# Softmax weights of a windowed attention: transposes on TensorE, or in blocks on VectorE with a way over DRAM

## The chip, the cores and the metric

The kernel runs on one core of a Trainium2 chip. The metric is the device time of one execution in microseconds (us). Lower is better.

## What is computed

One layer of a hybrid decoder block on 2048 tokens of width 1024, all in float32. A normalized input goes through one wide projection. One branch is a gated causal convolution of width 3. The other is attention over a sliding window of 128 tokens, with 16 query heads that share 4 key and value heads of 64 channels, and a learned sink for each head. Cut to the attention:

```
scores = einsum('bnqhgd,bnkhd->bnhgqk', qb, kb) * scale      # blocks of 128 queries, 256 keys
scores = where(valid, scores, NEG_INF)                       # 0 <= q_pos - k_pos < 128
m = maximum(max(scores, axis=-1), sink)
p = exp(scores - m)
p = p / (sum(p, axis=-1) + exp(sink - m))
out = einsum('bnhgqk,bnkhd->bnqhgd', p, vb)
```

Both branches are gated, projected and merged with sigmoid gates; an output projection and the residual follow.

## The kernel before

The tokens are worked in two tiles of 1024. In each tile the projections come one after the other: keys, values, queries, then the convolution's columns and its gate factor (the convolution stage), the merge gates (the gate stage), the two SiLU gates, and the projections of the two branches `ya` and `yb`. The output projection comes at the end. Each product is split into float32r high and low parts and summed on TensorE, with a scheme of sums that saves products, so a "unit" of 256 columns takes seven groups of 12 matmuls.

**Ticks.** Everything else hangs on these groups. The generators (`sunit`, `qunit`, `branch`) yield after each group, and `run` (L601) counts a tick for each yield. `put(n, f)` places a function at tick `n`. After each group `run` issues the next loads of weights, the high half of a piece of weights (ScalarE), the first two functions of the tick, the low half (VectorE), and then the rest of the tick's functions. Every engine works its own list strictly in the order in which this host program issues it. The order is fixed when the kernel is built; nothing is moved afterwards.

**An attention step** handles one of 4 key heads, one block of 128 queries, and the 4 query heads that belong to it. There are 32 steps in a token tile, 64 in all. Each has a place `n`, and `attention` (L1461) puts its parts at fixed distances from it:

- `att_load` (n - 4): SP loads queries `q`, keys `kq` and their low parts `lows`.
- `att_scores` (n): six matmuls into the one score buffer `s` (two PSUM banks), then masking and the row maximum on VectorE.
- `att_exp` and `att_load_v` (n + 1): exponentials on ScalarE, and the load of the values `v` by SP.
- `att_norm` (n + 2): VectorE divides by the sums. `p` now lies with the queries on the partitions.
- `att_turn` (n + 4): TensorE turns the four 128 by 128 blocks of `p` into the PSUM tile `pt` (L966). ScalarE copies `pt` twice (`xh` L969, `yp` L970), VectorE subtracts `xl = pt - xh`, and GpSimd cuts the window's triangles with four selections (`keep`, L979).
- `att_values` (n + 7): six matmuls with the values into `po` (L996).
- `att_out` (n + 8): ScalarE and VectorE add the halves in PSUM to `o` (L1007), and SP stores it.

The places of the first 16 steps are 5.25 ticks apart (rounded down) from the 48th tick of a token tile, and those of the other 16 are 3.25 ticks apart from the 129th. In the first token tile the convolution stage takes ticks 46 to 129 and the gate stage 130 to 185; the second token tile begins at tick 305.

**Buffers.** Most of these tiles come from one pool of 19 slots, `big`, each of 512 float32 for each partition (`slot`); a new tile takes a slot that became free, and its first writer waits for the last reader of the old one. `pt` and `po` come from three PSUM banks (`mbank`), which other transposes use too. GpSimd also issues DMAs (`nc.gpsimd.dma_start`); the other loads and stores are issued by SP in order.

VectorE's `transpose` is already in use in the query stage (`ptq<-q_t`), where it turns a 128 by 512 tile within blocks of 32 by 32.

Of the kernel before, what the change touches and what calls it, by code (L numbers as in the profile page):

```python
# [8 lines left out]
F32 = mybir.dt.float32  # L9
# [6 lines left out]
P = 128  # L16
# [8 lines left out]
G = NH // NKV  # L25
HD = 64
# [25 lines left out]
QUADS = [slice(32 * k, 32 * k + 32) for k in range(4)]  # L52

PE_TURNS = ((0, 0), (0, 1))
TURN_WAIT = 3
HALVES = (LH, UH)


@with_exitstack
def block_kernel(  # L60
# [12 lines left out]
    nc = tc.nc  # L73
# [16 lines left out]
    dram = ctx.enter_context(tc.tile_pool(name="dram", bufs=1, space=bass.MemoryType.DRAM))  # L90

    def slot(shape, dt, name):
        return big.tile(shape, dt, tag="big", name=name)
# [7 lines left out]
    def mbank(name):  # L101
        return ps_m.tile([P, HB, P], F32, tag="m", name=name)
# [31 lines left out]
    ident = consts.tile([P, P], F32, name="ident")  # L134
# [5 lines left out]
    for h in range(2):  # L140
        nc.gpsimd.affine_select(
            out=mask_f[:, h, :], in_=ones[:, 0:HD], pattern=[[1, HD]], compare_op=ALU.is_gt,
# [74 lines left out]
    vec = Woven()  # L217
# [23 lines left out]
    def add(o, a, b, eng=None):  # L241
        return (eng or vec).tensor_tensor(out=o, in0=a, in1=b, op=ALU.add)
# [355 lines left out]
    def put(n, f):  # L598
        at.setdefault(max(n, tick[0] + 1), []).append(f)

    def run(gen):  # L601
        while True:
            tick[0] += 1
            if next(gen, gen) is gen:
                tick[0] -= 1
                return
            ahead_loads()
            hi, lo = (piece() if tick[0] >= W_FROM else None) or (None, None)
            if hi:
                hi()  # L610

            fs = at.pop(tick[0], [])
            for f in fs[:2]:
                f()
            if lo:
                lo()
            for f in fs[2:]:
                f()
            vec.some(WOVEN)

# [338 lines left out]
        mul(p, p, st[:, 0].unsqueeze(2).to_broadcast([P, G, P]))  # L959
        return p  # L960

    def att_turn(t, j, b, p):
        nm = f"{t}_{j}_{b}"
        pt = mbank(f"pt{nm}")
        for i in range(G):
            nc.tensor.transpose(pt[:, i, :], p[:, i, :], ident)  # L966
        xh, xl = slot([P, G, P], F32R, f"xh{nm}"), slot([P, G, P], F32R, f"xl{nm}")
        y = slot([P, G, P], F32R, f"yp{nm}")
        nc.scalar.copy(xh, pt)  # L969
        nc.scalar.copy(y[LH], pt[UH])  # L970
        vec.tensor_tensor(out=xl, in0=pt, in1=xh.bitcast(F32), op=ALU.subtract)

        def keep(dst, src, prev):
            sg = 1 if prev else -1
            d4 = dst.rearrange("p g (e q) -> p (g e) q", q=HD)
            s4 = src.rearrange("p g (e q) -> p (g e) q", q=HD)
            nc.gpsimd.affine_select(  # L979
                out=d4, in_=s4, pattern=[[0, 2 * G], [-sg, HD]],  # L980
                compare_op=ALU.is_gt if prev else ALU.is_ge, fill=0.0, base=0,
                channel_multiplier=sg)

        keep(xh[UH], xh[UH], False)
        keep(y[LH], y[LH], True)
        keep(y[UH], xl[UH], True)
        keep(xl[UH], xl[UH], False)
        return xh, xl, y

    def att_values(t, j, b, pcv, v2):  # L990
        xh, xl, y = pcv
        po = mbank(f"po{t}_{j}_{b}").rearrange("p g q -> p (g q)")
        for h in range(2):
            cs = slice(h * 2 * P, (h + 1) * 2 * P)
            for n, (kind, xx) in enumerate(((2 + h, xh), (h, y), (2 + h, xl))):
                nc.tensor.matmul(  # L996
                    po[:, cs], lhsT=v2[:, kind, :], rhs=xx.rearrange("p g q -> p (g q)")[:, cs],
                    start=n == 0, stop=n == 2)
        return po

    def att_out(t, j, b, po):
        pov = po.rearrange("p (h c e q) -> p h c e q", h=2, c=2, e=2)
        o = slot([P, 2, P], F32, f"o{t}_{j}_{b}")
        for e in range(2):
            own, oth = HALVES[e], HALVES[1 - e]
            ov = o[own].rearrange("p c (h q) -> p h c q", h=2)
            nc.scalar.copy(ov, pov[oth, :, :, e, :])  # L1007
            add(ov, pov[own, :, :, e, :], ov)
        nc.sync.dma_start(
            od[t][2 * j : 2 * j + 2, :, b * P : (b + 1) * P].rearrange("c p q -> p c q"), o)  # L1010

# [449 lines left out]
    def attention(t, places):  # L1461
        for r, n in enumerate(places):
            j, b = divmod(r, NB)
            got = {}

            def step(k, f, got=got):
                def g():
                    got[k] = f(got)
                return g

            put(n - 4, step("l", lambda g, j=j, b=b: att_load(t, j, b)))
            put(n + 1, step("v", lambda g, j=j, b=b: att_load_v(t, j, b)))
            put(n, step("s", lambda g, j=j, b=b: att_scores(t, j, b, g["l"])))
            put(n + 1, step("e", lambda g, j=j, b=b: att_exp(t, j, b, g["s"])))
            put(n + 2, step("n", lambda g: att_norm(g["e"])))
            put(n + 4, step("x", lambda g, j=j, b=b: att_turn(t, j, b, g["n"])))
            put(n + 7, step("o", lambda g, j=j, b=b: att_values(t, j, b, g["x"], g["v"])))
            put(n + 8, step("z", lambda g, j=j, b=b: att_out(t, j, b, g["o"])))

    def next_tile(t, n0):  # L1480

# [53 lines left out]
    for t in range(NT):  # L1535
        ops = state[t]["ops"]
        ys, yc, opa, opb = {}, {}, {}, {}
        t0 = tick0
        if t == 0:
            t0 += 1  # L1540
        attention(t, [t0 + 48 + int(5.25 * r) for r in range(16)] + [
            t0 + 129 + int(3.25 * r) for r in range(16)])
        if t > 0:
            run(sunit(("k", t), ops, fin_k(t)))
            run(sunit(("v", t), ops, fin_v(t)))
        for j in range(NKV):
            if t == j == 0:
                run(qunit(("q", t, j), ops, fin_q(t, j)))
            else:
                run(sunit(("q", t, j), ops, fin_q(t, j), t == 0 and j < Q_TWO))  # L1550
        for k in range(KC):
            run(sunit(("cv", t, k), ops, fin_cv(t, k, ys)))
            if k % 2:
                run(sunit(("b", t, k // 2), ops, fin_b(t, k // 2, ys)))
        for w, key in enumerate(("ga", "gb")):
            for j in range(NJ):
                run(sunit((key, t, j), ops, fin_g(t, w, j)))

        def use_o(k, q, o):
            nc.sync.dma_start(ocd[t][k, :, hs(q)], o)  # L1560

        def oa_form(k, q):
            opa[k, q] = split_op(yc[k, q], f"opa{t}_{k}_{q}")

        def use_y(k, q, y):
            yc[k, q] = y
            if k >= KC - 2:
                oa_form(k, q)

        zs = [("za", j) + fin_z(t, j, od[t], "za", use_o) for j in range(NJ)]  # L1570
        zs += [("z", j) + fin_z(t, j, yd[t], "z", use_y) for j in range(NJ)]
        zs[0][3]()
        for n, (key, j, fin, _) in enumerate(zs):
            if n + 1 < len(zs):
                put(tick[0] + 4, zs[n + 1][3])
            else:

                for i, (k, q) in enumerate([(k, q) for q in (1, 0) for k in range(KC - 2)]):
                    put(tick[0] + 1 + i // 2, lambda k=k, q=q: oa_form(k, q))
            run(sunit((key, t, j), ops, fin))  # L1580
        n0 = tick[0]
        for n, (k, q) in enumerate((k, q) for q in range(2) for k in range(KC)):
# [74 lines left out]
```

## Time and profile before

| | us |
|---|---|
| median of 3 runs (lowest to highest) | 1988.09 (1986.5 to 1989.5) |
| the profiled execution | 1987.95 |
| its span, first to last instruction | 1986.2 |
| TensorE busy in it | 1964.9 (99%) |
| VectorE busy | 1407.5 (71%) |
| ScalarE busy | 927.4 (47%) |
| GpSimd busy | 379.4 (19%) |

The profile is of one execution. PE is TensorE's matmuls, PEld its weight loads, DVE is VectorE, ACT is ScalarE, POOL is GpSimd and SP the engine that issues most DMAs; SPq is its queue. A line such as `L966 PE MATMUL pt<-ident,p` names the source line, the engine, the operation, and what is written from what. Behind it stand the shapes, the count, the busy time, the mean duration in nanoseconds and the idle time ahead of it with what ended it. In a timeline the first two columns are the start and the duration, or for several merged instructions the stretch that they take. Matmuls are pipelined: the next one starts before the last one's recorded end, so the pitch from start to start is what TensorE spends on one. A window row gives the stretch, its length, each engine's busy time and count, TensorE's granted clock, the share of the DMA engines and their GB/s.

### The profile page before, as it was taken

To read this page: it belongs to the slowest core of one execution; us is meant where nothing else is said; L and a number is where in the kernel's file an instruction comes from. 1 tells how busy PE (TensorE), PEld (TensorE's weight loads), DVE (VectorE), ACT (ScalarE), POOL (GpSimd) and SP (SyncE) were. 2 spreads that over 40 slices of the span, in tenths; PEclk is the share of its full clock that TensorE was granted. 3 is DMA by queue.
4 is the path that set the end of the run, shared out by engine and by line. 5 is a ranking of instruction groups with operands and counts; after the bars stand their busy time and mean duration, and the time that the engine had idled before them with its cause. 6 is when DMAs were issued, how large, how long until landed. Compare 5 with 4: busy or idle time off the path is not lost.

```text
span 1986.2 us, 27039 instructions
## 1 busy us (share of the span) xinstructions
PE 1964.9 (99%) x9102; PEld 1631.9 (82%) x9102; DVE 1407.5 (71%) x2428; ACT 927.4 (47%) x1860; POOL 379.4 (19%) x530
## 2 busy tenths in 40 slices
PE   9999999999999999999999999999999999999999
PEld 7877888888888888888878888887888888888887
DVE  7988788787775554379689778876776565356654
ACT  7655545556664343324555544555664334222321
POOL 2372122223230000110463222222321000100000
PEclk9999999999999999999999999999999999999999
DMA  8484543465555435774584544364654524855553
GB/s 295 109 221 124 154 125 112 133 185 184 174 158 201 137 110 185 265 270 143 144 216 136 154 119 123 117 189 155 200 181 162 185 96 157 271 190 172 163 175 112
DMA packets 204059, 332.95 MB, mean 168 GB/s; under 512 B 24144, under 2 KB 98896, under 8 KB 203920
## 3 DMA queue, kind: packets, MB, share of 16 engines
q1 hardware_dynamic: 189696, 288.96, 45.7%
q0 software_dynamic: 14080, 42.22, 7.9%
q8 instruction: 73, 1.20, 0.3%
q14 instruction: 66, 0.54, 0.1%
q10 hardware_dynamic: 144, 0.03, 0.0%
HBM read 234.39 MB, written 96.73 MB: 167 GB/s over the span
## 4 chain that ended last, share of the span: by engine, by line
PE 82%; DVE 7%; ACT 4%; DMA 3%; issue 2%; POOL 1%; SPq 0%; DVEq 0%; ACTq 0%; POOLq 0%
PE Y L410 26%; PE yb L1126 9%; PE ya L1126 8%; PE Vcv L410 4%; PE Xcv L410 4%; PE Vb L410 2%; PE Xb L410 2%; PE Xz L410 2%; PE Xza L410 2%; PE Vo L410 2%; PE Xo L410 2%; PE Vza L410 2%; PE po L996 2%; PE Vz L410 2%; PE Xgb L410 2%
## 5 line engine op out<-in xcount | busy, mean ns | idle before, releaser
L979 POOL TENSOR_SCALAR_AFFINE_SELECT xh<-xh 64x512 fp32r<-64x512 f32 x64 | 70.6, 1103 | 652.3 <-DVE xl L211 499.6
L950 ACT ACTIVATE p<-s,st,rq 128x128 f32<-128x128 f32 x256 | 113.3, 453 | 0.5
L211 DVE TENSOR_TENSOR o<-po,o 64x256 f32<-64x256 f32 x128 | 53.7, 420 | 58.0 <-ACT o L1007 55.7
L211 DVE SCALAR_TENSOR_TENSOR tha<-tha,ya 128x512 f32<-128x512 f32 x32 | 22.0, 687 | 97.6 <-PE ya L1126 94.6
L1007 ACT COPY o<-po 64x256 f32<-64x256 f32 x128 | 46.9, 367 | 83.8 <-DVE o L211 82.3
L211 DVE TENSOR_TENSOR xl<-pt,xh 128x512 fp32r<-128x512 f32 x64 | 44.2, 691 | 53.9 <-ACT yp L970 48.4
L1126 PE MATMUL ya<-opa,wya_1h 128*128 128x512 f32 x256 | 79.6, 391 | 0.9 <-ACT opa L238 0.5
L410 PE MATMUL Xcv<-oph,wcv_ah 128*128 128x512 f32 x256 | 79.7, 392 | 0.0
L1126 PE MATMUL yb<-opb,wyb_1h 128*128 128x512 f32 x256 | 78.9, 389 | 0.0
L1126 PE MATMUL yb<-opb,wyb_0h 128*128 128x512 f32 x256 | 78.9, 389 | 0.0
L1126 PE MATMUL ya<-opa,wya_0h 128*128 128x512 f32 x256 | 78.8, 389 | 0.0
L238 ACT CAST opb<-ocr 128x512 fp32r<-128x512 f32 x32 | 19.9, 621 | 110.6 <-DMA ocr<-ocd 109.0
L1126 PEld LDWEIGHTS ya<-opa,wya_1h 128*128 128x128 f32 x256 | 48.0, 188 | 12.2 <-ACT opa L238 1.3
L1126 PEld LDWEIGHTS ya<-opa,wya_0h 128*128 128x128 f32 x256 | 48.0, 188 | 10.0
L1126 PEld LDWEIGHTS yb<-opb,wyb_1h 128*128 128x128 f32 x256 | 48.0, 188 | 9.9
L1126 PEld LDWEIGHTS yb<-opb,wyb_0h 128*128 128x128 f32 x256 | 48.0, 188 | 9.9
L410 PEld LDWEIGHTS Xcv<-oph,wcv_ah 128*128 128x128 f32 x256 | 47.2, 188 | 9.3
L979 POOL TENSOR_SCALAR_AFFINE_SELECT yp<-xl 64x512 fp32r<-64x512 f32 x64 | 54.0, 844 | 3.1
L211 DVE SCALAR_TENSOR_TENSOR thb<-thb,yb 128x512 f32<-128x512 f32 x32 | 21.9, 686 | 43.7 <-PE yb L1126 43.0
L211 DVE SCALAR_TENSOR_TENSOR y<-u,cols,y 128x512 f32<-128x512 f32 x64 | 49.1, 767 | 5.4 <-ACT y L1038 4.2
L969 ACT CAST xh<-pt 128x512 fp32r<-128x512 f32 x64 | 37.5, 586 | 32.5 <-PE pt L966 31.7
L1214 POOL DMA_DIRECT2D wo<-in_w_out x16 | 8.7, 541 | 225.0 <-DVE opb L211 205.6
(590 smaller groups left out, 6260.2 us busy)
## 6 DMA issues: line engine op xcount, KB each, us to landing
wcv_raw<-in_w_in SPq DMA_DIRECT2D x32, 512.0 KB, 4.4
q<-q2d SPq DMA_DIRECT2D x64, 256.0 KB, 3.9
v<-vd SPq DMA_DIRECT2D x128, 128.0 KB, 3.3
gd<-th SPq DMA_DIRECT2D x64, 256.0 KB, 2.3
wq_raw<-in_w_in SPq DMA_DIRECT2D x16, 512.0 KB, 5.2
q2d<-q_h POOLq DMA_DIRECT2D x64, 128.0 KB, 4.7
q2d<-q_l POOLq DMA_DIRECT2D x64, 128.0 KB, 4.6
kq<-q2d SPq DMA_DIRECT2D x128, 64.0 KB, 3.6
```

The source lines that it names most:

```text
L211: r = f(*args, **kw)
L238: nc.scalar.copy(hi, src)
L410: nc.tensor.matmul(ps, lhsT=w[:, j, :], rhs=b[:, m, :], start=start and j == 0 and i == 0, stop=j == KP - 1 and i == 2, skip_group_check=n ...
L950: nc.scalar.activation(out=p[:, i, :], in_=sg[:, i, HD : 3 * HD], func=AF.Exp, bias=st[:, 1, i : i + 1], scale=rv[:, i // 2, i % 2 : i % 2 ...
L969: nc.scalar.copy(xh, pt)
L979: nc.gpsimd.affine_select(out=d4, in_=s4, pattern=[[0, 2 * G], [-sg, HD]], compare_op=ALU.is_gt if prev else ALU.is_ge, fill=0.0, base=0, ...
L996: nc.tensor.matmul(po[:, cs], lhsT=v2[:, kind, :], rhs=xx.rearrange("p g q -> p (g q)")[:, cs], start=n == 0, stop=n == 2)
L1007: nc.scalar.copy(ov, pov[oth, :, :, e, :])
L1126: nc.tensor.matmul(ps, lhsT=w[:, j, cs], rhs=o[:, m, :], start=n == 0 and i == 0, stop=n == KC - 1 and i == 2)
L1214: nc.gpsimd.dma_start(h, w_o[c * P : (c + 1) * P, hs(q)])
```

## The change

The four TensorE transposes of `att_turn` go. In their place come two new steps. `att_flip` lets VectorE turn `p` into `f` within blocks of 32 by 32, with the four heads side by side in each block row, and GpSimd sends `f` to DRAM. `att_back` lets GpSimd read it back with four DMAs, one for each 32 partitions, in such an order that the blocks change places and `x` has the keys on the partitions. `att_turn` then works on `x` in SBUF instead of `pt` in PSUM. The columns of `x` are ordered by block of 32 queries, head and query, and the patterns in `keep`, `att_values` and `att_out` follow that order.

The steps get new distances: loads at n - 5, block transpose at n + 2, the way back at n + 5, the value loads at n + 6, `att_turn` at n + 9, the value matmuls at n + 13, the output at n + 14. The places change as well: in the convolution stage 0, 6, 10 and 15 ticks into every 21, in the gate stage 3.75 ticks apart. And `run` issues one function of a tick ahead of the low half of weights instead of two.

```diff
+V_, F_, B_, X_, O_ = 6, 2, 5, 9, 13
...
             fs = at.pop(tick[0], [])
-            for f in fs[:2]:
+            for f in fs[:1]:
                 f()
             if lo:
                 lo()
-            for f in fs[2:]:
+            for f in fs[1:]:
                 f()
...
+    def att_flip(t, j, b, p):
+        nm = f"{t}_{j}_{b}"
+        f = slot([P, G * P], F32, f"f{nm}")
+        vec.transpose(out=f, in_=p.rearrange("p g (b r) -> p b g r", r=32))
+        fd = dram.tile([P, G * P], F32, name=f"fd{nm}")
+        nc.gpsimd.dma_start(fd, f)
+        return fd
+
+    def att_back(t, j, b, fd):
+        x = slot([P, G, P], F32, f"x{t}_{j}_{b}")
+        src = fd.rearrange("(a r) (b x) -> b r a x", a=4, b=4)
+        for k in range(4):
+            nc.gpsimd.dma_start(x[QUADS[k]], src[k])
+        return x
+
+    def att_turn(t, j, b, pt):
+        nm = f"{t}_{j}_{b}"
-        pt = mbank(f"pt{nm}")
-        for i in range(G):
-            nc.tensor.transpose(pt[:, i, :], p[:, i, :], ident)
...
-                out=d4, in_=s4, pattern=[[0, 2 * G], [-sg, HD]],
+                out=d4, in_=s4, pattern=[[0, 2], [-32 * sg, 2], [0, G], [-sg, 32]],
...
-                    po[:, cs], lhsT=v2[:, kind, :], rhs=xx.rearrange("p g q -> p (g q)")[:, cs],
+                    po[:, cs], lhsT=v2[:, kind, :], rhs=xx[:, :, h * HD : (h + 1) * HD],
...
-            put(n - 4, step("l", lambda g, j=j, b=b: att_load(t, j, b)))
-            put(n + 1, step("v", lambda g, j=j, b=b: att_load_v(t, j, b)))
+            put(n - 5, step("l", lambda g, j=j, b=b: att_load(t, j, b)))
+            put(n + V_, step("v", lambda g, j=j, b=b: att_load_v(t, j, b)))
...
-            put(n + 4, step("x", lambda g, j=j, b=b: att_turn(t, j, b, g["n"])))
-            put(n + 7, step("o", lambda g, j=j, b=b: att_values(t, j, b, g["x"], g["v"])))
-            put(n + 8, step("z", lambda g, j=j, b=b: att_out(t, j, b, g["o"])))
+            put(n + F_, step("f", lambda g, j=j, b=b: att_flip(t, j, b, g["n"])))
+            put(n + B_, step("b", lambda g, j=j, b=b: att_back(t, j, b, g["f"])))
+            put(n + X_, step("x", lambda g, j=j, b=b: att_turn(t, j, b, g["b"])))
+            put(n + O_, step("o", lambda g, j=j, b=b: att_values(t, j, b, g["x"], g["v"])))
+            put(n + O_ + 1, step("z", lambda g, j=j, b=b: att_out(t, j, b, g["o"])))
...
-        attention(t, [t0 + 48 + int(5.25 * r) for r in range(16)] + [
-            t0 + 129 + int(3.25 * r) for r in range(16)])
+        attention(t, [t0 + 48 + 21 * (r // 4) + (0, 6, 10, 15)[r % 4] for r in range(16)] + [
+            t0 + 129 + int(3.75 * r) for r in range(16)])
```

More of the change, by code (lines that the diff above doesn't have):

```diff
@@ L960, in att_norm @@
         return p
-    def att_turn(t, j, b, p):
+    def att_flip(t, j, b, p):
         nm = f"{t}_{j}_{b}"
-        pt = mbank(f"pt{nm}")
-        for i in range(G):
-            nc.tensor.transpose(pt[:, i, :], p[:, i, :], ident)
+        f = slot([P, G * P], F32, f"f{nm}")
[11 more added lines that the diff above has]
+        nm = f"{t}_{j}_{b}"
         xh, xl = slot([P, G, P], F32R, f"xh{nm}"), slot([P, G, P], F32R, f"xl{nm}")
@@ L976, in keep @@
             sg = 1 if prev else -1
-            d4 = dst.rearrange("p g (e q) -> p (g e) q", q=HD)
-            s4 = src.rearrange("p g (e q) -> p (g e) q", q=HD)
+            d4 = dst.rearrange("p (e s) (g q) -> p e s g q", s=2, q=32)
+            s4 = src.rearrange("p (e s) (g q) -> p e s g q", s=2, q=32)
             nc.gpsimd.affine_select(
-                out=d4, in_=s4, pattern=[[0, 2 * G], [-sg, HD]],
+                out=d4, in_=s4, pattern=[[0, 2], [-32 * sg, 2], [0, G], [-sg, 32]],
                 compare_op=ALU.is_gt if prev else ALU.is_ge, fill=0.0, base=0,
@@ L1001, in att_out @@
     def att_out(t, j, b, po):
-        pov = po.rearrange("p (h c e q) -> p h c e q", h=2, c=2, e=2)
+        pov = po.rearrange("p (h e s c q) -> p h e s c q", h=2, e=2, s=2, c=2)
         o = slot([P, 2, P], F32, f"o{t}_{j}_{b}")
@@ L1005, in att_out @@
             own, oth = HALVES[e], HALVES[1 - e]
-            ov = o[own].rearrange("p c (h q) -> p h c q", h=2)
-            nc.scalar.copy(ov, pov[oth, :, :, e, :])
-            add(ov, pov[own, :, :, e, :], ov)
+            ov = o[own].rearrange("p c (h s q) -> p h s c q", h=2, s=2)
+            nc.scalar.copy(ov, pov[oth, :, e])
+            add(ov, pov[own, :, e], ov)
         nc.sync.dma_start(
```

## The prediction

> **What bounds the kernel now.** I read the head of the page first, then the windows cut at the stages that hold attention, then the timeline of TensorE around one attention step, and last the waits.
>
> ```profile
> span 1986.2 us, 27039 instructions
> PE 1964.9 (99%) x9102; PEld 1631.9 (82%) x9102; DVE 1407.5 (71%) x2428; ACT 927.4 (47%) x1860; POOL 379.4 (19%) x530
> ```
>
> TensorE is busy in 99% of the span, and the time is the length of its instruction stream plus the few places where it stands still. An instruction taken out of that stream shortens the kernel by its own pitch; work added on another engine costs only where it makes TensorE wait.
>
> ```profile
> core 0: us, PE busy (x) PEld busy (x) DVE busy (x) ACT busy (x) POOL busy (x), PEclk, DMA share, GB/s
> 143.30:409.00 265.70, 262.32 (x1255) 219.30 (x1254) 219.66 (x402) 132.45 (x306) 62.59 (x89) 0.99 0.45 131
> 409.00:598.10 189.10, 186.89 (x941) 158.04 (x940) 142.70 (x268) 121.63 (x301) 57.74 (x68) 1.00 0.58 176
> 1048.10:1308.80 260.70, 260.17 (x1250) 217.57 (x1248) 218.40 (x392) 133.43 (x304) 59.66 (x74) 1.00 0.45 131
> 1308.80:1501.40 192.60, 189.37 (x941) 159.46 (x940) 141.56 (x267) 119.61 (x298) 58.18 (x68) 0.99 0.58 177
> ```
>
> These are the convolution stage and the gate stage of each token tile; nearly all 64 attention steps lie in them. VectorE is the second limit: 219.66 us of 265.70 us, 83%, in the convolution stage, 75% in the gate stage. ScalarE, GpSimd (24% and 31%) and the DMA engines have room.
>
> **The change part by part.**
>
> *Four TensorE transposes leave each step.* The timeline of TensorE around the first set:
>
> ```profile
> 171.07 0.39 PE L410 MATMUL Xcv<-oph,wcv_al 128*128 128x512 f32 x1
> 171.30 0.60 PE L966 MATMUL pt<-ident,p 128*128 128x128 f32 x4
> 171.66 0.71 PE L410 MATMUL Vcv<-oph,wcv_sh 128*128 128x512 f32 x2
> 172.21 0.40 PE L410 MATMUL Vcv<-oph,wcv_sl 128*128 128x512 f32 x1
> 172.44 0.62 PE L410 MATMUL Vcv<-oph,wcv_sh 128*128 128x512 f32 x2
> 172.90 0.39 PE L410 MATMUL Vcv<-oph,wcv_sl 128*128 128x512 f32 x1
> ```
>
> I count from start to start, because durations overlap. 171.07 to 171.30 is one product matmul, 0.23 us. The four transposes take 171.30 to 171.66, 0.36 us. The next two products take 0.55 us (to 172.21) where the same pair then takes 0.46 us (172.44 to 172.90), so the switch back costs 0.09 us. That is 0.45 us a step and 64 x 0.45 = 28.8 us. The bounds are 64 x 0.36 = 23.0 us, if the switch stays, and the busy time of the group below, 38.4 us, which counts overlap.
>
> ```profile
> L966 PE MATMUL pt<-ident,p 128*128 128x128 f32 x256 | 38.4, 272 | 2.3 <-DVE p L211 2.3
> ```
>
> The matmuls that remain for scores and values keep count and columns; the values only read 64-column runs, and the scores already read runs out of a wider tile, so I cost that at nothing.
>
> *The first load of a tile stands one tick earlier.* Before, SP sent the first `q` at 135.57 and then stood until VectorE's transposes had freed a slot of `q_t`; TensorE paid for it:
>
> ```profile
> SPq L881 <- DVE ptq L211: 16.8, 1, 16.8
> ...
> 135.57 0.33 SPq L875 DMA_DIRECT2D q<-q2d  x1
> 152.78 1.58 SPq L881 DMA_DIRECT2D kq<-q2d  x2
> ...
> 155.85 0.39 PE L410 MATMUL Xcv<-oph,wcv_al 128*128 128x512 f32 x1
> 158.01 0.30 PE L921 MATMUL s<-lows,kq 128*128 128x128 f32 x1 [1.76 <-DMA lows<-kd]
> 159.46 1.00 PE L410 MATMUL Y<-oph,wcv_th 128*128 128x512 f32 x2
> 160.25 0.63 PE L410 MATMUL Y<-oph,wcv_tl 128*128 128x512 f32 x1
> ...
> 162.81 0.45 PE L410 MATMUL Y<-oph,wcv_tl 128*128 128x512 f32 x1
> ```
>
> 155.85 to 158.01 is 2.16 us where 0.23 is usual: 1.9 lost. After it the pace is half: the eight matmuls from 159.46 to 162.81 take 3.35 us in place of 8 x 0.23 = 1.84, 1.5 lost. In the changed order this tile takes the place of a key tile that GpSimd sent out eight ticks before, so the 17 us wait goes: 3.4 us. If another slot holds it up, nothing is gained. In the second tile the load has no such stall, before or after. All later loads of queries and keys also move one tick ahead, the value loads five ticks later, now seven ahead of their use. In the gate stage the loads reuse slots that TensorE frees in the tick before; SP stands there for up to one tick, with weight loads behind it, and those are covered by the two units that are loaded ahead. I cost this at nothing; uncovered it is one of the 0.7 us stalls below for each step.
>
> *Waits of the transposes go with them.* TensorE waited for the normalized weights twice, both in the gate stage:
>
> ```profile
> 535.02 0.28 PE L996 MATMUL po<-xl,v 128*128 128x256 f32 x1
> 535.85 0.63 PE L966 MATMUL pt<-ident,p 128*128 128x128 f32 x4 [0.55 <-DVE p L211]
> ...
> 1361.81 0.28 PE L996 MATMUL po<-xl,v 128*128 128x256 f32 x1
> 1363.87 0.63 PE L966 MATMUL pt<-ident,p 128*128 128x128 f32 x4 [1.78 <-DVE p L211]
> ...
> 1365.71 1.11 PE L410 MATMUL Y<-oph,wga_sh 128*128 128x512 f32 x2
> 1366.61 0.63 PE L410 MATMUL Y<-oph,wga_sl 128*128 128x512 f32 x1
> ```
>
> The first lost 0.83 - 0.12 = 0.7 us. The second lost 1.9 us, and half pace follows again (0.90 us for two matmuls at 1365.71), which I put at the 1.5 us of the place above. Together 4.1 us. Next late in these places is the score matmul, which waits for ScalarE to read the one score buffer:
>
> ```profile
> PE s L921 <- ACT p L950: 2.9, 6, 1.3
> ```
>
> Steps 3.75 ticks apart in place of 3.25 can only ease this: between 0 and 2.9 us, taken as 0.
>
> *VectorE gets a transpose and loses a wait.*
>
> ```profile
> L211 DVE STREAM_TRANSPOSE ptq<-q_t 128x512 f32<-128x512 f32 x24 | 17.1, 717 | 0.0
> L211 DVE TENSOR_TENSOR xl<-pt,xh 128x512 fp32r<-128x512 f32 x64 | 44.2, 691 | 53.9 <-ACT yp L970 48.4 <-DMA q<-q2d 1.7 <-PE Y L410 1.5
> ```
>
> The nearest row is the same block transpose of a 128x512 tile, 0.72 us: 64 x 0.72 = 46 us. The subtraction `xl` stood 48.4 us for ScalarE's second copy out of the same PSUM bank. Its operands now lie in SBUF, and in the built program it waits for the first copy alone. Busy and forced idle time together stay level, so TensorE loses nothing here; if the wait stays, VectorE in the convolution stage goes from 83% to (219.66 + 16 x 0.72) / 258.5 = 89%.
>
> [...]
>
> *GpSimd gets five DMA issues a step, and ScalarE and VectorE wait for the last landing.*
>
> ```profile
> L772 POOL DMA_DIRECT2D q2d<-q_h x64 | 44.2, 690 | 38.4 <-ACT q_t L503 18.8 <-ACT q_h L767 13.5 <-DMA kd<-k_h 2.9
> L979 POOL TENSOR_SCALAR_AFFINE_SELECT xh<-xh 64x512 fp32r<-64x512 f32 x64 | 70.6, 1103 | 652.3 <-DVE xl L211 499.6 <-issue 64.6 <-PE Y L410 38.8
> L979 POOL TENSOR_SCALAR_AFFINE_SELECT xl<-xl 64x512 fp32r<-64x512 f32 x64 | 47.9, 749 | 4.4
> ...
> q2d<-q_h POOLq DMA_DIRECT2D x64, 128.0 KB, 4.7
> h<-in_xt POOLq DMA_DIRECT2D x16, 256.0 KB, 8.6
> ```
>
> 5 x 0.69 = 3.5 us beside four selections of 0.75 to 1.10, some 3.4 us: 7 us of GpSimd for each step of 11 to 16 us. Capacity is no bound; the order is. One late step of the gate stage before:
>
> ```profile
> 475.28 0.44 PE L921 MATMUL s<-lows,kq 128*128 128x384 f32 x1
> 483.90 0.69 DVE L211 TENSOR_TENSOR xl<-pt,xh 128x512 fp32r<-128x512 f32 x1 [0.82 <-ACT yp L970]
> 488.66 0.69 DVE L211 TENSOR_TENSOR p<-p,st 128x512 f32<-128x512 f32 x1
> 490.91 0.59 ACT L969 CAST xh<-pt 128x512 fp32r<-128x512 f32 x1 [1.76 <-PE pt L966]
> ```
>
> Counted from its scores, normalizing ends at 14.1 and ScalarE's copy stands at 15.6, at place n + 4. The stage has 56 ticks, so a tick becomes (189.10 - 17 x 0.45) / 56 = 3.2 us, and the copy, five ticks later, comes near 31. On the way there: block transpose to 14.8, issue 0.69, landing 4.7: 20.2. The way back has its place at n + 5, 16 us. Where the step before stands four ticks ahead, that step's four selections lie in the same tick and first in GpSimd's queue. They wait for its subtraction, which runs some 4 to 5 us behind its tick (483.90 is a late one), so they end near 24.8. Four issues end at 27.6, and the last landing is at 32.3: some 1.4 us after ScalarE wants it. In the convolution stage normalizing ends near 11, and only one place in four is so close; there it lands in time.
>
> While ScalarE waits for `x`, the copies out of TensorE's banks (L428) and the high halves of weights stand behind it; on VectorE, waiting in `xl`, the low halves and the bank additions. One product matmul group of 2.7 us lies between a bank's end and the need for its copy, so most of 1.4 us is covered. The bounds are 0 and 32 steps x 1.4 = 45 us (24 gate steps and 8 convolution steps lie so close). I take one in four, 8 steps, with the 0.7 us of the row at 535.02: 5.6 us, since the nearest rows show that lateness of this kind passed TensorE by in most steps.
>
> The two ways also move 2 x 256 KB a step: 15 steps x 0.52 = 7.9 MB on 176 GB/s x 189 us = 33 MB in a gate stage, so the DMA share goes from 0.58 to about 0.72, an estimate by bytes. Loads of weights land more than a unit ahead; nothing is added for them.
>
> *The sum.* The profiled execution took 1987.95 us, 1.8 us over its span and 0.1 us under the median of 1988.09. 1987.95 - 28.8 - 3.4 - 4.1 + 5.6 = 1957.3 us.
>
> **The rivals.**
>
> *The chain eats half.* The same mechanism, with the stall at TensorE in all 32 close steps and 0.7 us each, 22 us in place of 5.6: 1951.7 + 22.4 = 1974 us. For it: the two waits at L966 show that gate steps do run late. Against: ScalarE is busy only 64% there.
>
> *All is given back.* The 32 close steps stall TensorE by 1.1 us each, 36 us, as much as leaves: 1951.7 + 36 = 1988 us. Here the way over DRAM is worth what the transposes cost; for and against it speaks what speaks for the half. [...]
>
> *VectorE becomes the bound (slower).* Its idle time in the convolution stage is 46 us. If that is all hand-over time that no queue can fill, and the `xl` wait stays, the stage lasts 265.7 + 16 x 0.72 = 277 us, 11.5 us more, in both tiles. With the gate stages 2 x 17 x 0.45 = 15 us shorter, 3.4 + 4.1 gained and 5.6 lost, 1988 + 23 - 15 - 2 = 1994 us. It decides from the point where VectorE's busy and forced idle time exceed 258 us in that stage. Against it: the idle time holds the wait that goes.
>
> *The return lands too late (slower).* If `x` lands in 8.6 us as the `h` loads of the same queue did, it comes 1.4 + 3.9 = 5.3 us late; 2.7 us are covered, 2.6 us reach TensorE in 32 steps: 83 us, 1951.7 + 83 = 2035 us. For it: the gate stage's DMA share rises. Against: those loads were bursts of many in a row, and the page's other row is 4.7 us. [...]
>
> **How the numbers follow.** The forecast has 0.58, its own range 1948 (2.9 us gained at the scores too, nearly no new stall) to 1966; half eaten 0.18; all given back 0.04; VectorE bound 0.11; too late 0.09. The range for 8 in 10 takes in the forecast, the half, the tie and the lower part of VectorE's case: 1947 to 1992. A difference under 0.2%, 4 us, can hardly be told from none. Faster 0.58 + 0.18 = 0.76, same 0.04, slower 0.11 + 0.09 = 0.20.
>
> **What would show it.** TensorE's list without the transposes and 0.23 us across those places shows the first step right; SP sending the first `kq` directly behind `q`, the second; a group of block transposes near 0.72 us and an `xl` without the wait for `yp`, the third. The chain is right if ScalarE's `xh` waits little for the DMA of `x`; `xh <- DMA x` high in the waits, with waits of TensorE for ScalarE's bank copies, would mean the late return. VectorE near 95% in the convolution stage would mean the VectorE case. It is wrong outright if the convolution stage is not shorter by some 7 us.

## The result, and the profile after

| | before | after |
|---|---|---|
| median (lowest to highest), 4 runs each | 1987.38 (1986.5 to 1989.5) | 2003.82 (2001.73 to 2007.75) |
| ratio, 95% interval | | 1.0083 (1.0064 to 1.0103) |
| profiled execution, its span | 1987.95, 1986.2 | 2005.35, 2003.6 |

The change made the kernel slower by 16 us, 0.8%, and the interval of the ratio lies above 1. The prediction was 1957.3 us, and its range of 1947 to 1992 us does not hold the result.

The head of the page after, and the windows cut at the same stages as before (convolution and gate stage of the first tile, then of the second):

```profile
span 2003.6 us, 27366 instructions
PE 1952.2 (97%) x8846; PEld 1607.5 (80%) x8846; DVE 1447.8 (72%) x2492; ACT 931.7 (47%) x1862; POOL 556.3 (28%) x850
```

```profile
142.90:403.50 260.60, 255.56 (x1184) 209.87 (x1183) 223.65 (x408) 131.88 (x301) 98.40 (x154) 1.00 0.55 160
403.50:591.20 187.70, 180.32 (x853) 149.33 (x852) 144.47 (x268) 114.68 (x280) 93.79 (x137) 0.99 0.72 214
...
1045.10:1325.60 280.50, 262.56 (x1183) 215.31 (x1183) 226.87 (x402) 130.14 (x297) 92.55 (x141) 0.97 0.50 148
1325.60:1508.50 182.90, 178.09 (x849) 147.67 (x849) 142.72 (x261) 112.61 (x273) 92.08 (x135) 1.00 0.71 215
```

TensorE has 256 instructions fewer (9102 before), but it is busy 97% of a longer span. The two convolution stages do the same work, and one got shorter (265.7 to 260.6 us) while the other got longer (260.7 to 280.5 us), at a granted clock of 0.97. So the largest loss is not an even load on an engine: it sits at places of the second tile. (The experiments find an even loss beside it.) The largest of TensorE's waits, over the whole span, and then the waits in the second convolution stage alone (waiting engine and line, releaser, us in total, times, longest):

```profile
PE Y L412 <- DVE Vcv L213: 13.2, 7, 3.8
```

```profile
POOL fd L972 <- DVE f L213: 89.2, 12, 14.2
...
ACT y L1055 <- POOL u L1050: 29.6, 8, 4.8
DVE o L213 <- ACT o L1024: 16.1, 18, 3.4
...
PE Y L412 <- DVE Vcv L213: 13.2, 7, 3.8
```

All 13.2 us of it fall into this one stage. The clock adds at most (1 - 0.97) x 280.5 = 8.4 us, somewhat less because its mean also counts time in which TensorE stands anyway. Together that is up to 21.6 us, about what the stage lasts too long. Three times, some 73 us apart (from 1140.88, 1213.90 and 1286.53), TensorE stands for 3.8 us. The first, engine by engine (start, duration, engine, line, operation; in brackets the idle time and its releaser):

```profile
1137.23 0.58 POOL L972 DMA_DIRECT2D fd<-f  x1 [7.58 <-DVE f L213]
1137.86 0.18 POOL L1050 COPY u<-halo 128x2 f32<-128x2 f32 x1
...
1138.08 1.34 ACT L1055 ACTIVATE y<-u,cols 128x512 f32<-128x512 f32 x2 [2.60 <-POOL u L1050]
1139.32 0.56 ACT L439 COPY s5cv<-Vcv 128x512 f32<-128x512 f32 x1
1139.91 0.37 ACT L1024 COPY o<-po 64x256 f32<-64x256 f32 x1
...
1136.22 0.71 DVE L213 STREAM_TRANSPOSE f<-p 128x512 f32<-128x512 f32 x1
1140.31 0.42 DVE L213 TENSOR_TENSOR o<-po,o 64x256 f32<-64x256 f32 x1 [3.37 <-ACT o L1024]
...
1141.80 0.69 DVE L213 TENSOR_TENSOR xl<-x,xh 128x512 fp32r<-128x512 f32 x1 [0.21 <-ACT xh L986]
1142.41 1.90 DVE L213 SCALAR_TENSOR_TENSOR y<-u,cols,y 128x512 f32<-128x512 f32 x2
1144.34 0.70 DVE L213 TENSOR_TENSOR Vcv<-s5cv,Y 128x512 f32<-128x512 f32 x1
...
1140.88 0.39 PE L412 MATMUL Xcv<-oph,wcv_al 128*128 128x512 f32 x1
1145.09 1.22 PE L412 MATMUL Y<-oph,wcv_th 128*128 128x512 f32 x2 [3.82 <-DVE Vcv L213]
1146.11 0.63 PE L412 MATMUL Y<-oph,wcv_tl 128*128 128x512 f32 x1
1146.53 1.06 PE L412 MATMUL Y<-oph,wcv_th 128*128 128x512 f32 x2
1147.38 0.63 PE L412 MATMUL Y<-oph,wcv_tl 128*128 128x512 f32 x1
```

Read from the top: GpSimd stands 7.58 us at the new write of `f`, in its own queue, for VectorE's transpose. Behind it in that queue stands a copy of 0.18 us that has nothing to do with attention: the convolution's *edge* step. At the tick after a convolution unit, `fin_cv` lets GpSimd put two columns in front of `u` (a memset in the first tile, L1048; a copy from `halo` in the second, L1050), and then ScalarE scales `u` into `y` (L1055). So ScalarE waits 2.60 us for this copy, with its copies out of PSUM behind it; VectorE waits 3.37 us for one of those; and VectorE's addition `Vcv`, for which TensorE stands, comes behind `o`, `xl` and the taps on `y`. After the stop two matmuls take 0.85 us (1146.53 to 1147.38) in place of 0.46.

Why only the second tile? Its convolution stage begins two ticks sooner after the tile's first tick, but the places of the steps are counted from that first tick in both. So the same distance `n + 2` puts the flip (the block transpose and the write of `f`) of one step in four on the very tick of the edge there, and two ticks before it in the first tile.

A smaller loss stands at the end of the second gate stage, whose last steps run into the SiLU stage: there ScalarE and VectorE wait for the return of `x`, and weights come late (ScalarE and VectorE above, TensorE below):

```profile
1548.94 0.62 ACT L986 CAST xh<-x 128x512 fp32r<-128x512 f32 x1 [5.95 <-DMA x<-fd]
...
1549.60 0.69 DVE L213 TENSOR_TENSOR xl<-x,xh 128x512 fp32r<-128x512 f32 x1 [3.69 <-ACT xh L986]
...
1554.31 0.73 PE L412 MATMUL Vza<-oph,wza_sh 128*128 128x512 f32 x2 [0.83 <-ACT wza_sh L308]
1557.27 0.79 PE L412 MATMUL Vza<-oph,wza_sl 128*128 128x512 f32 x1 [2.23 <-DVE wza_sl L213]
...
1558.71 0.63 PE L412 MATMUL Vza<-oph,wza_sl 128*128 128x512 f32 x1
1559.14 1.05 PE L412 MATMUL Vza<-oph,wza_sh 128*128 128x512 f32 x2
```

### The profile page after: what moved, and what is told of

Same layout as the page of the kernel before. It is cut to its first block, busy times and chain, and to the rows that moved or that the text cites. A ratio compares the mean times of both kernels' runs of the same rounds, so it can differ in the third digit from the quotient of the medians.

```text
span 2003.6 us, 27366 instructions
## 1 busy us (share of the span) xinstructions
PE 1952.2 (97%) x8846; PEld 1607.5 (80%) x8846; DVE 1447.8 (72%) x2492; ACT 931.7 (47%) x1862; POOL 556.3 (28%) x850
## 4 chain that ended last, share of the span: by engine, by line
PE 53%; DVE 21%; DMA 8%; issue 6%; ACT 6%; POOL 3%; SPq 1%; DVEq 0%; POOLq 0%; ACTq 0%
PE Y L412 16%; PE yb L1143 9%; PE ya L1143 8%; DVE st L213 2%; PE Vo L412 2%; PE Xo L412 2%; PE Xz L412 2%; PE Vza L412 2%; PE Vz L412 2%; ACT p L952 2%; PE Xza L412 2%; DVE y L213 2%; DVE wcv_raw L213 1%; DMA x<-fd 1%; PE Xga L412 1%
## 5 line engine op out<-in xcount | busy, mean ns | idle before, releaser
L979 POOL DMA_DIRECT2D x<-fd x256 | 140.1, 554 | 47.7 <-DMA fd<-f 23.6
L996 POOL TENSOR_SCALAR_AFFINE_SELECT xh<-xh 64x512 fp32r<-64x512 f32 x64 | 63.0, 985 | 261.2 <-DVE xl L213 169.3
L972 POOL DMA_DIRECT2D fd<-f x64 | 37.0, 578 | 252.0 <-DVE f L213 181.1
L213 DVE TENSOR_TENSOR xl<-x,xh 128x512 fp32r<-128x512 f32 x64 | 43.9, 687 | 35.4 <-ACT xh L986 30.0
L521 POOL DMA_DIRECT2D x<-in_x x8 | 4.3, 540 | 201.4 <-PE ya L1143 200.6
L412 PE MATMUL Y<-oph,wcv_th 128*128 128x512 f32 x128 | 45.5, 440 | 13.2 <-DVE Vcv L213 13.2
```

The lines of the kernel that those rows point to most:

```text
L213: r = f(*args, **kw)
L412: nc.tensor.matmul(ps, lhsT=w[:, j, :], rhs=b[:, m, :], start=start and j == 0 and i == 0, stop=j == KP - 1 and i == 2, skip_group_check=n ...
L521: eng.dma_start(xt, x2[r0 : r0 + P, :])
L972: nc.gpsimd.dma_start(fd, f)
L979: nc.gpsimd.dma_start(x[QUADS[k]], src[k])
L996: nc.gpsimd.affine_select(out=d4, in_=s4, pattern=[[0, 2], [-32 * sg, 2], [0, G], [-sg, 32]], compare_op=ALU.is_gt if prev else ALU.is_ge, ...
```

## The experiments

Four theories. **A**: small edge copies on GpSimd stand behind issues that wait for VectorE, where both fall on one tick. **B**: `x` comes back too late. **C**: VectorE's extra 46 us are paid on the path. **D**: gate places 3.75 ticks apart push attention's tail into the SiLU stage.

Lengths of the stages in the profiled executions, in us, each from the first matmul of a projection to that of the next. The other stages differ by at most 3 us. A kernel that builds on another one is marked.

| | conv. 1 | gates 1 | SiLU 1 | conv. 2 | gates 2 | SiLU 2 | median |
|---|---|---|---|---|---|---|---|
| before | 265.7 | 189.0 | 76.2 | 260.7 | 192.6 | 76.9 | 1987.4 |
| after | 260.6 | 187.8 | 80.0 | 280.5 | 182.9 | 87.2 | 2003.8 |
| e1 edge on ScalarE | 258.2 | 185.8 | 80.0 | 263.5 | 182.3 | 87.5 | 1984.5 |
| e2 tile 2 shifted by -2 | 261.4 | 184.3 | 80.0 | 260.3 | 183.3 | 86.0 | 1984.4 |
| e3 tile 1 shifted by +2 | 290.9 | 192.3 | 80.0 | 279.8 | 183.5 | 86.1 | 2039.3 |
| e4 no block transpose | 255.3 | 182.0 | 80.0 | 276.2 | 178.5 | 85.7 | 1983.5 |
| e5 = e1 + e2 | 258.5 | 185.8 | 80.0 | 257.3 | 183.1 | 86.3 | 1978.6 |
| e6 = e5, way back at n + 4 | 261.7 | 184.7 | 80.0 | 260.7 | 183.1 | 86.3 | 1980.6 |
| e7 = before, no TensorE transposes | 258.9 | 184.5 | 76.2 | 253.3 | 183.8 | 76.9 | 1961.1 |
| e8 = e1, no way over DRAM | 258.2 | 181.7 | 80.0 | 256.4 | 181.6 | 80.9 | 1968.0 |
| e9 = e5, gate places 3.5 ticks apart | 258.3 | 201.7 | 86.4 | 258.0 | 185.5 | 80.3 | 1999.8 |
| e9 = e5, gate places 3.25 ticks apart | 258.2 | 197.8 | 77.7 | 257.3 | 195.0 | 79.7 | 1992.1 |
| e10 = e5, no block transpose | 254.2 | 180.8 | 80.0 | 253.2 | 178.9 | 87.1 | 1962.6 |
| e12 = e5, loads of `x` by SP | 258.4 | 183.2 | 80.0 | 257.1 | 182.8 | 80.9 | 1971.0 |

The medians of before beside these runs were 1986.8 to 1987.1 us. The profiled execution of e6 was the longest of its five, 4 us above their median.

**The edge's copies on ScalarE.**

```diff
-                nc.gpsimd.memset(u[:, 0:2], 0.0)
+                nc.scalar.activation(out=u[:, 0:2], in_=cols[:, 0:2], func=AF.Copy, scale=0.0)
...
-                nc.gpsimd.tensor_copy(u[:, 0:2], halo[:, k, :])
+                nc.scalar.copy(u[:, 0:2], halo[:, k, :])
...
-                nc.gpsimd.tensor_copy(halo[:, k, :], u[:, 2 * H :])
+                nc.scalar.copy(halo[:, k, :], u[:, 2 * H :])
```

> The changed kernel, with the convolution's edge work (two columns of u filled from zero or halo, two columns of halo saved) on ScalarE instead of GpSimd. Theory A, that these small GpSimd copies stand in GpSimd's queue behind the new DMA issues and selections, which wait for VectorE, and that ScalarE's scaling of y, the bank copies behind it and in the end TensorE wait for them: the second tile's convolution stage falls from 280.5 us to about 256, the whole from 2003.8 to about 1979 us, and the waits of ScalarE's y for GpSimd's u (43 us) go. Theory B, that x lands too late for ScalarE's copy: that stage stays within 3 us of 280, the whole at 2001 to 2006. Theory C, that VectorE's added work is the bound: the same as B.

Measured: 1984.45 us, ratio to before 0.9991 (0.9982 to 1.0001). Three tiny copies of each unit, moved to another queue, gave back 19 us, 17.0 of them in the second convolution stage. TensorE's wait fell:

```profile
PE Y L412 <- DVE Vcv L213: 5.1, 5, 1.4
```

A is shown in kind, but it had expected 256 us for the stage and 1979 for the whole. The stage is still some 6 us above that of e5 (below), so the tick remains crowded for other reasons too.

**Only the places of the second tile, two ticks earlier.**

```diff
-        attention(t, [t0 + 48 + 21 * (r // 4) + (0, 6, 10, 15)[r % 4] for r in range(16)] + [
+        attention(t, [t0 + 48 - 2 * t + 21 * (r // 4) + (0, 6, 10, 15)[r % 4] for r in range(16)] + [
```

> The changed kernel, with the second tile's attention places in the convolution stage two ticks earlier, so that they stand to its units as they do in the first tile. Theory A: the write of f no longer shares its tick with the edge copies; the second tile's convolution stage falls from 280.5 to about 260 us as in the first tile, the whole to about 1984 us. Theories B and C: distances between the parts of a step and VectorE's work are the same, so the stage stays within 4 us of 280 and the whole within 2000 to 2006.

Measured: 1984.43 us, 0.9988 (0.9979 to 0.9998), the second convolution stage 260.3 us: the first tile's figure, as A expected. No work is changed here, only the places, by two ticks.

**The opposite: the first tile's places two ticks later.**

```diff
+        attention(t, [t0 + 48 + 2 * (1 - t) + 21 * (r // 4) + (0, 6, 10, 15)[r % 4] for r in range(16)] + [
```

> The changed kernel, with the first tile's attention places in the convolution stage two ticks later, so that they stand to its units as they do in the second tile. Theory A: the first tile's convolution stage rises from 260.6 to about 280 us, the whole to about 2022 us. Theories B and C: that stage stays within 4 us of 260.6 and the whole within 2000 to 2008.

Measured: 2039.32 us, 1.0265 (1.0248 to 1.0282). The loss can be made in the first tile at will: its convolution stage went from 260.6 to 290.9 us. The wait that was 13.2 us in after is now 26.0 us in sum, 12.9 of them in the first tile's stage. A single late load, at 423 us and still in that stage, adds 8.6 us; without it the stage is near the 280 us expected. The whole is 17 us above the 2022 us expected; beside this load, the first gate stage is 4.5 us longer than in after:

```profile
PE Y L412 <- DVE Vcv L213: 26.0, 13, 3.8
...
PE s L923 <- DMA lows<-kd: 8.6, 1, 8.6
```

**No transposes on VectorE.**

```diff
-        f = slot([P, G * P], F32, f"f{nm}")
-        vec.transpose(out=f, in_=p.rearrange("p g (b r) -> p b g r", r=32))
...
-        nc.gpsimd.dma_start(fd, f)
+        nc.gpsimd.dma_start(fd, p.rearrange("p g q -> p (g q)"))
```

> The changed kernel without VectorE's 64 block transposes: p itself goes to DRAM, so the weights are used in a wrong arrangement; all DMAs, waits and places stay. Theory C: 46 us of VectorE work go, and each convolution stage gives back 8 to 12 us, the whole is near 1980 us. Theory A: the write still waits for VectorE's normalization, 0.7 us earlier, so each of the 3 to 6 worst places gives back 0.7 us, the whole is 1996 to 2002 us. Theory B: the return lands 0.7 us earlier, the whole is 1994 to 2002 us.

Measured: 1983.52 us, 0.9984 (0.9974 to 0.9993). Where A and B alone expected little, 20 us came back: 5.3, 5.8, 4.3 and 4.4 us, evenly over the four stages. The second convolution stage is still 276.2 us, so this is another loss than A's. C holds in kind, with half the 8 to 12 us that it expected in each convolution stage, and with as much again in the gate stages.

**Edge and shift together.**

> The changed kernel with both remedies: the edge work on ScalarE, and the second tile's convolution places two ticks earlier. Theory A, that one cause (edge copies behind GpSimd's waits) made the stage slow and each remedy alone takes most of it away: the second tile's convolution stage comes to about 258 us, as the first tile's with the edge work on ScalarE; the whole about 1979 us. Rival: the two do not add, the stage stays at 260 to 263 and the whole at 1982 to 1986.

Measured: 1978.57 us, 0.9958 (0.9943 to 0.9973): faster than the kernel before. The second convolution stage, 257.3 us at a granted clock of 1.00, is now as good as the first:

```profile
144.30:402.70 258.40, 254.06 (x1183) 210.17 (x1182) 226.09 (x408) 133.46 (x317) 98.42 (x138) 1.00 0.56 162
1042.50:1299.70 257.20, 254.20 (x1183) 210.33 (x1182) 225.13 (x404) 133.40 (x308) 96.31 (x135) 1.00 0.55 159
```

From after to this, 25.2 us: what A costs. The two remedies gave 19 us each when alone, so they overlap.

**The way back one tick earlier.**

```diff
-V_, F_, B_, X_, O_ = 6, 2, 5, 9, 13
+V_, F_, B_, X_, O_ = 6, 2, 4, 9, 13
```

> Both remedies, and the way back one tick earlier (n + 4 in place of n + 5), so that its DMA issues stand ahead of the step before's four selections in GpSimd's queue. Theory B, that x lands too late in the gate stages and behind them: the 32 us that ScalarE's xh waits for x fall below 10, the 7 us stall in the SiLU gate stage after the second tile's gates goes, and the whole is 6 to 12 us below the kernel with both remedies, about 1970 us. Rival: GpSimd then stands for the landing of f with the selections behind it, the values come late, and the whole is the same or up to 6 us slower.

Measured: 1980.58 us, 0.9965 (0.9951 to 0.9979), 2 us above e5 with overlapping intervals. ScalarE's wait for `x` went from 25.3 to 4.9 us, but GpSimd paid for it in its queue; its wait for `f` to land was 23.9 us in e5 and is now

```profile
POOL x L979 <- DMA fd<-f: 44.0, 15, 5.9
```

Sending the loads earlier from the same queue only moved the wait. The stall in the second SiLU stage did not go, against theory B: there the last step's `x` still comes 2.8 us late, and the stage stays at 86.3 us.

**The kernel before without its 256 TensorE transposes.**

```diff
-        pt = mbank(f"pt{nm}")
-        for i in range(G):
-            nc.tensor.transpose(pt[:, i, :], p[:, i, :], ident)
+        pt = p
```

> The kernel before without the 256 TensorE transposes: ScalarE and VectorE take p itself in place of the turned tile, so the weights are used unturned; places and all other work stay. What the transposes cost, alone: by the forecast's terms 28.8 us of pitch and 4.1 us of waits, so about 1954 us (1950 to 1959). If their time were covered by other waits, 1965 or more.

Measured: 1961.11 us, 0.987 (0.9855 to 0.9885). The transposes and their waits are worth 25.7 us by the medians (27.3 by the profiled spans), not 32.9. The waits at the scores grew when they went (2.9 us, 6 times, and 1.8 us, once, before):

```profile
PE s L921 <- ACT p L950: 5.7, 10, 1.3
PE s L921 <- DMA lows<-kd: 4.0, 4, 2.0
```

**No way over DRAM** (the edit is on top of e1).

```diff
-        fd = dram.tile([P, G * P], F32, name=f"fd{nm}")
-        nc.gpsimd.dma_start(fd, f)
-        return fd
+        return f.rearrange("p (g q) -> p g q", g=G)
...
-        x = slot([P, G, P], F32, f"x{t}_{j}_{b}")
-        src = fd.rearrange("(a r) (b x) -> b r a x", a=4, b=4)
-        for k in range(4):
-            nc.gpsimd.dma_start(x[QUADS[k]], src[k])
-        return x
+        return fd
```

> The changed kernel with the edge work on ScalarE and without the way over DRAM: att_turn takes f, turned in blocks that keep their places, straight from SBUF; VectorE's transposes and all places stay, and the blocks stand wrong. Theory B, late return: the waits of xh go, with the 7 us in the SiLU gate stage and some in the gate stages, 1984.5 falls to 1970 to 1976 us. Theory C, VectorE's load: the stalls stay where they are, 1980 to 1985 us.

Measured: 1968.03 us, 0.9904 (0.9889 to 0.9918): 16.4 us under e1. The parts are 6.6 us in the second SiLU stage, which is the late return shown above, 4.1 in the first gate stage, and 7.1 in the second convolution stage, most of which the shift of e5 gives as well (6.2). So B is right for some 10 us while the block transposes stand.

**Gate places closer together, 3.5 and 3.25 ticks** (on top of e5).

```diff
-            t0 + 129 + int(3.75 * r) for r in range(16)])
+            t0 + 129 + int(3.5 * r) for r in range(16)])
```

> The kernel with both remedies, with the gate stage's attention places 3.5 ticks apart in place of 3.75, so that the last step ends 4 ticks sooner and less of it reaches into the SiLU gate stage. Theory D, that the steps' tail stands against the loads of that stage in the pool of slots and in SP's queue: the second tile's SiLU gate stage for attention falls from 86 to 78 to 82 us, the gate stages take 2 to 4 us more for the steps that move into them, and the whole falls from 1978.6 by 2 to 6 us. Rival: the gate stages cannot hold the steps closer together, and the whole is 0 to 6 us slower.

> The same with places 3.25 ticks apart, as in the kernel before; the last step ends 8 ticks sooner. Theory D: the SiLU gate stages come to 76 to 78 us, the whole to 1971 to 1977. Rival, the pool of slots and VectorE's load at that spacing: stalls of TensorE for the row of scores and the bank additions grow, the whole is at 1980 to 1990.

Measured: 1999.82 us, 1.0063 (1.0048 to 1.0078), and 1992.09 us, 1.0028 (1.0018 to 1.0038). The second SiLU stage did fall from 86.3 to 80.3 and 79.7 us, as far as D said with 3.5 and less far with 3.25. But with 3.5 the first SiLU stage rose from 80.0 to 86.4 us, with one wait of 5.1 us there, and the first gate stage, 185.8 us in e5, came to 201.7 and 197.8, and with 3.25 the second came to 195.0. The limit differs: with 3.5 TensorE waits for VectorE (the first row), with 3.25 for ScalarE to read the score buffer (the second):

```profile
PE Y L412 <- DVE th L213: 11.9, 6, 4.7
```

```profile
PE s L923 <- ACT p L952: 13.2, 11, 1.9
```

D fails as a whole: in e5 the wider places are worth more than their tail costs. The growth of the first SiLU stage by 3.8 us from before to after is largely work that moved there: 24 of the value matmuls lie in it, with 3.50 us of TensorE's time, and one before.

**No transposes on VectorE, in e5** (the edit of e4).

> The kernel with both remedies and without VectorE's 64 block transposes (p itself goes to DRAM, so the weights are used in a wrong arrangement). On the changed kernel itself leaving them out gave 20 us back, more than theory A allowed. Theory C, VectorE's load costs by itself: again 12 to 20 us, 1959 to 1967. If they cost so much only because they stood ahead of the write that GpSimd waited for, 1972 to 1977.

Measured: 1962.55 us, 0.9873 (0.9858 to 0.9888), 16.0 us under e5: C with A's loss out of the way. Again each of the four stages got 4 to 5 us shorter. Over these four stages their length less TensorE's busy time is 18.4 us in e5 and 7.5 us here. The waits at TensorE that go are small ones, for work that stands in VectorE's queue; the largest in e5 are

```profile
PE Vcv L412 <- DVE wcv_sl L213: 4.2, 8, 1.6
PE Y L412 <- DVE th L213: 3.9, 3, 2.2
PE Vcv L412 <- DVE y L213: 2.4, 4, 0.7
```

and of the same kind in e10

```profile
PE Vcv L412 <- DVE wcv_sl L213: 2.2, 2, 1.6
...
PE Y L412 <- DVE th L213: 1.2, 1, 1.2
```

The edit also saves the slot of `f` in each step. That this is what helps was not tested by itself, but in e5 VectorE stands at most 0.13 us before any of its 64 block transposes, so none of them waits for a slot.

**The loads of `x` issued by SP** (on top of e5).

```diff
-            nc.gpsimd.dma_start(x[QUADS[k]], src[k])
+            nc.sync.dma_start(x[QUADS[k]], src[k])
```

> The kernel with both remedies, with the four loads of x issued by SP in place of GpSimd. Theory B: they no longer stand behind GpSimd's selections and land sooner, ScalarE's waits for x (25 us) fall below 8; SP stands for the landing of f with weight loads behind it. If the late landing is what is left, the whole falls by 4 to 10 us to 1969 to 1975; if SP's queue is tighter than GpSimd's, it is 2 to 15 us slower.

Measured: 1971.04 us, 0.9914 (0.9898 to 0.9931), the best complete version: 16 us under the kernel before and 33 under the change as it was made. The second SiLU stage fell from 86.3 to 80.9 us, as without the way over DRAM, and VectorE's wait for `xh` in `xl` from 23.4 to 12.3 us. The loads no longer queue behind selections that wait for `xl`: from the end of the write's issue to the first load's issue it is 7.4 us on the mean in e5 and 5.4 us here. The issues and landings were shorter as well (medians 551 to 430 ns and 3.8 to 3.1 us), and this run does not separate the two. The whole is 7.5 us shorter than in e5.

## Why the prediction was wrong, step by step

The medians give an account, each figure a difference of two runs (before is the 1986.8 us measured beside e5 and e7). The steps are not independent (see the end of this section), so in another order the middle two would come out otherwise:

| step | us | median |
|---|---|---|
| before | | 1986.8 |
| TensorE's transposes and their waits go (e7) | -25.7 | 1961.1 |
| way over DRAM, new places and first load, edge and tick mended (e10) | +1.4 | 1962.6 |
| block transposes on VectorE (e5) | +16.0 | 1978.6 |
| edge copies in GpSimd's queue on the flip's tick (after) | +25.2 | 2003.8 |

**GpSimd's queue: wrong, the largest miss (25 us).** "Capacity is no bound; the order is" was the right sentence, and the list made from it was not complete. The step worked out what `x` waits for and stopped there. It did not list everything that stands behind a waiting issue on that engine, so it put that at nothing; the edge copies stand there. The trace of before had the warning: ScalarE already waited for these copies, in both tiles (the waits of ScalarE, before), though TensorE passed that time without a stop.

```profile
ACT y L1038 <- POOL u L1031: 15.7, 4, 4.3
ACT y L1038 <- POOL u L1033: 15.6, 4, 3.9
```

Nor did the step work out the places by tile; the two tiles differ by two ticks, and that decided. None of the rivals was this. The mark that the prediction set itself, a convolution stage some 7 us shorter, came to -5.1 us in the first tile and +19.8 in the second.

**VectorE "level, costs nothing": wrong by 16 us (e10 to e5), by less without the way over DRAM.** The duration was right, and the old wait for the second copy did go. But 30.0 us of wait for the first copy came in place of the 48.4 (the group in after):

```profile
L213 DVE TENSOR_TENSOR xl<-x,xh 128x512 fp32r<-128x512 f32 x64 | 43.9, 687 | 35.4 <-ACT xh L986 30.0
```

More important, the sum of busy and idle time is the wrong measure. VectorE is busy 81% to 86% of the convolution stages, and each 0.71 us inserted ahead of the low half of some weights or of a bank addition can reach TensorE: 16.0 us of 64 x 0.71 = 45 us did. This is near the VectorE rival's mechanism, hand-over time that no queue fills, at about a third of what was put on the engine. The rival's stage of 277 us was reached (280.5), but only in the second tile and for another reason.

**Transposes: right in kind, 7 us too much.** 28.8 + 4.1 = 32.9 us forecast, 25.7 measured on the same chip. Part of the difference shows at the scores, which the forecast had as "next late" and took as 0: in e7 their two waits grew from 4.7 to 9.7 us. The 4.1 us also hold 1.5 us of half pace, read from one profiled execution; single executions of before, beside e1, go from 1985.0 us at a mean granted clock of 1.0 to 1989.2 us at 0.997, so not each of them has it.

**First load: right in kind.** Its 3.4 us were not measured alone. SP sends `kq` directly behind `q`, and TensorE's first scores wait for nothing:

```profile
129.10 1.67 SPq L877 DMA_DIRECT2D q<-q2d  x1
130.95 1.95 SPq L883 DMA_DIRECT2D kq<-q2d  x2
...
155.69 0.22 PE L923 MATMUL s<-lows,kq 128*128 128x128 f32 x1
```

**Late return, 5.6 us: too small.** The working has a slip: by its own ticks ScalarE's copy comes at 15.6 + 5 x 3.24 = 31.8 us and not "near 31", so `x` would have been 0.5 us late and not 1.4. The durations erred on the safe side (690 ns an issue and 4.7 us a landing were assumed), and still `x` came late (a group, the DMA issues and the waits of after):

```profile
L979 POOL DMA_DIRECT2D x<-fd x256 | 140.1, 554 | 47.7 <-DMA fd<-f 23.6
...
fd<-f POOLq DMA_DIRECT2D x64, 256.0 KB, 4.0
x<-fd POOLq DMA_DIRECT2D x256, 64.0 KB, 3.8
...
ACT xh L986 <- DMA x<-fd: 32.2, 13, 5.9
```

The working had 32 close steps late. The trace has 13 waits of 2.5 us on the mean and up to 5.9: fewer and longer, so less is covered. The price is some 10 us (e5 against e8; 7.5 by e12), and the largest piece, about 7 us, lies in the SiLU stage, which the working did not look at although the last steps reach into it. The "too late" rival's slow landings did not happen: 3.8 us at the median, in place of its 8.6. The issues took 551 to 576 ns, beside a VectorE that was busy 77% to 86% in these stages.

**DMA share: right**, 0.72 and 0.71 in the gate stages.

**The terms are not independent.** Each with the new places and against e7, the block transposes without the way over DRAM cost 6.9 us (e8), the way without the transposes 1.4 us (e10; a net figure, because e10 also gains the first load), and both together 17.5 us (e5). So the 16 us and the 10 us above share some 9 us and must not be added. e8 lacks the shift of places, but its second convolution stage, 256.4 us, shows no loss from that. Why 9 us arise only from the two together was not taken apart further; that the transpose stands at the head of the chain whose end is late would give this, and is argued, not shown.

## What to carry to other kernels

When an instruction that must wait is put into an engine's queue, list every instruction that can stand behind it there, however small and unrelated, and follow who waits for those, for each phase of the loop by itself. A queue with idle time did not hide the waits here, because urgent work shared it (GpSimd was busy 28%): putting 0.18 us copies on another queue was worth 19 us, moving places by two ticks 19, and giving four issues to another queue 7. Nor was an engine at 85% beside a bottleneck at 99% free: 16.0 of the 45 us put on VectorE came back as small waits.

## What the runs showed of the hardware that was not expected

- GpSimd's selections with the longer pattern took longer: the median for `xl` went from 658 to 760 ns (the line's instructions, before and after; minimum, median and maximum). The pattern is what changed in them, though no run changes it alone. The prediction kept the old durations:

```profile
L979 POOL TENSOR_SCALAR_AFFINE_SELECT xl<-xl x64: 657/658/1659, 176.7 to 1506.1; 64x512 fp32r<-64x512 f32 x64
```

```profile
L996 POOL TENSOR_SCALAR_AFFINE_SELECT xl<-xl x64: 759/760/1282, 190.3 to 1553.8; 64x512 fp32r<-64x512 f32 x64
```

- A stop of TensorE could cost more than its length: after 3.82 us the pitch was 0.43 us in place of 0.23 (1146.11 to 1146.53), at a granted clock of 0.50 from 1145 to 1149, and the stage with three such stops had a mean granted clock of 0.97. Shorter stops were followed by it too: after the waits of 0.83 and 2.23 us up to 1557.27 the pitch was the same 0.43 us (1558.71 to 1559.14). The length of a stop does not decide alone: the one of 1.76 us at the first scores of before (158.01) was followed by half pace (0.43 us from 160.25 to 160.68), and the one of 1.96 us in the query stage of after (81.94) by the full pace (0.23 us from 82.51 to 82.74, granted clock 1.00 from 80 to 88).
